# Low parts of weight chunks: an adding DMA in place of a subtraction, in one part of a dense fp32 kernel

## The chip, the cores and the metric

The kernel runs on one core of a Trainium2 chip. The metric is the device time of one execution in microseconds; lower is better. Three runs of the kernel before gave 2870.39 to 2872.4 us, median 2871.46 us.

## The reference

The reference sends 512 tokens of 1024 features through two blocks of two layers each, all in float32:

```
h = concat(meta, x)                            # 16 + 512 tokens
for l in (0, 1):                               # block 1
    z = rms_norm(h) @ w_in                     # projections
    ya = sliding-window attention with sinks (16 heads, window 128) * silu(gate)
    ym = mLSTM, 4 heads, normed, * sigmoid(o) * silu(gate)
    h = h + concat(ya, ym) @ w_out
x = h[16:]
for l in (0, 1):                               # block 2
    z = rms_norm(x) @ w_in_2
    a = differential attention, 8 heads; b = dilated attention, 3 groups of 4 heads
    c = attention over 256 memory tokens, 4 heads
    x = x + (gated sum of a, b, c through their own matrices) @ w_out_2
out = rms_norm(x) * g_final
```

Nearly all the arithmetic is in the products with the weights. They are needed to float32's precision.

## The kernel before

Features lie on the partitions and tokens along the free dimension. TensorE multiplies in float32r, a shorter form of float32, so each operand is taken as a sum of a high part (the value rounded to float32r) and a low part (what is left). A product is the sum of three: high times high, high times low, low times high.

A weight chunk is a tile of 128 partitions by 1024 words (512 KB), which serves 8 blocks of 128 by 128. There are 404 of them, and `weights()` prepares each one. SP loads the raw chunk (`wr`, two tiles in rotation), ACT casts it to the high part (`wh`, three tiles), and the low part (`wl`, three tiles) is raw minus high: on POOL for every third chunk (L184), on DVE for the others (L171, through `split`). `dense()` then runs, for a chunk, first the 16 steps that use `wh` and then the 8 that use `wl`; the steps have 512 columns in block 2 and two halves of 264 in block 1. `dense_tok()` does the same with the chunk as the moving operand.

A layer of block 1 has 50 chunks for its projections (`w1`) and 16 for its output (`wo1`). A layer of block 2 has 32 chunks up to the end of the differential heads, 40 for the dilated heads, and then 65 for the memory attention, the gates, the branch matrices and the output.

The attention's own pieces (scores, softmax, transposes, weighted values, evacuations) are generators that advance by a stage after every dense product. A scheduler in the framework then orders each engine's instructions by a timeline of its own; each engine runs its list in that order, and waits at an instruction whose inputs or whose buffer are not there yet. So an engine's list holds weight work and attention work mixed, and what stands behind a waiting instruction waits with it.

Names that come up: L458 and L957 score plus mask and its maximum (DVE), L470 and L986 the exponentials (ACT), L478, L989 and L990 the scaled weights (DVE), L486 and L943 their transposes (PE), L174 and L329 evacuations of PSUM (DVE), L1245/L1246 copies of key halves and L1007 squares (POOL).

Of the kernel before, what the change touches and what calls it, by code (L numbers as in the profile page):

```python
# [10 lines left out]
F32 = mybir.dt.float32  # L11
# [10 lines left out]
# attention of block 1: queries in blocks of 112, each sees 16 meta keys and a window of 240  # L22
# [4 lines left out]
# the order of the groups of four heads and of the mLSTM's heads  # L27
ORDER = [("a", 0), ("m", 0), ("a", 1), ("m", 1), ("a", 2), ("m", 2), ("a", 3), ("m", 3)]
# blocks of tokens of the mLSTM
# [4 lines left out]
# the evacuation of a product goes before this many instructions that were given earlier  # L34
AHEAD = 300
# rounds of the streams for each dense product: block 1's, its output projection's, block 2's (differential, other)
# [6 lines left out]
# the table of per-feature values and of rows that all partitions need  # L43
# [14 lines left out]
def turned(t):  # L58
    """the tokens of each tile in reverse order."""
    return tiles4(t)[:, :, ::-1]  # L60


class Kernel:
    def __init__(self, nc, tc, d, es):
# [12 lines left out]
        self.nw = 0  # chunks of weights so far  # L77

    # ------------------------------------------------------------ storage
# [4 lines left out]
    def slot(self, dt=F32, shape=None):  # L84
        """one of the slots of 528 words for each partition; release() names the last use."""
        i = self.idle.popleft()
        t = self.sp.tile(shape or [128, L1], dt, name=self.uid("s"), tag=f"s{i}")
        self.held[id(t)] = (i, t)
        return t
# [27 lines left out]
    # ------------------------------------------------------------ a software pipeline  # L117
    # What follows a dense product (posts) and the attention's pieces (units, in streams) are generators.
    # They advance by stages after every dense product, so that a stage's inputs are there when its turn comes.
    def post(self, gen):  # L120
        """starts now and goes on by a stage at every step."""
        self.posts.append(gen)
        self.advance(self.posts, [gen])
# [12 lines left out]
    def round(self, s):  # L136
        """the stream's active units go on by a stage, and the next one starts."""
# [14 lines left out]
    def drain(self, gens=None):  # L152
        """until these units have been through (None: all posts)."""
# [8 lines left out]
    # ------------------------------------------------------------ products  # L162
# [3 lines left out]
    def split(self, src, hi, lo, scale=None):  # L166
        """src * scale = hi + lo, both exact in float32r."""
# [8 lines left out]
    def weights(self, src):  # L176
        w = lambda tag, dt: self.wp.tile([128, 1024], dt, name=self.uid(tag), tag=tag, bufs=2 if tag == "wr" else 3)
        raw = w("wr", F32)
        self.nc.sync.dma_start(raw, src)
        hi, lo = w("wh", F32R), w("wl", F32R)  # L180
        self.nw += 1
        if self.nw % 3 == 1:
            self.nc.scalar.copy(hi, raw)  # L183
            self.nc.gpsimd.tensor_tensor(lo, raw, hi.bitcast(F32), ALU.subtract)  # L184
        else:
            self.split(raw, hi, lo)
        return hi, lo

    def dense(self, outs, chunks, xs, halves, ks=None):
        """outs[j] = sum over k of W_k^T x_k on the columns halves[j]: hi hi + hi lo + lo hi."""  # L190
# [8 lines left out]
    def dense_tok(self, chunks, xs, nt, vh, vl, rc):  # L199
        """256 columns of the product with tokens on partitions, scaled by rc, in two parts."""  # L200
# [13 lines left out]
    def rms_rows(self, r, acc, T, halves, n, exp=True):  # L214
        """r = 1/sqrt(acc summed over the partitions / n + eps), the same on all partitions; its log without exp."""
# [12 lines left out]
    def rsqrt(self, y, x, shape):  # L228
        """y = 1/sqrt(x) of small tiles: a guess from the exponent, then Newton's steps."""
# [10 lines left out]
    def columns(self, r, rc, n):  # L240
        """rc[t, i] = r[0, 128 i + t]; r is the same on all partitions."""
# [16 lines left out]
    def layer_input(self, st, m, x, T, g):  # L258
        """what the next layer needs of tile m of the residual: its parts times the gain, its squares."""
# [5 lines left out]
    def keep(self, name, m, x, T):  # L265
        """the residual waits in memory for the end of the layer."""
# [4 lines left out]
    def silu2(self, z, T):  # L271
        """z = 2 * silu(z)."""
# [6 lines left out]
    # ------------------------------------------------------------ constants  # L279
    def constants(self):  # L280
# [30 lines left out]
        # the mLSTM's first 16 tokens: the values' high | low | high parts at 0, 32, 64 with a column of ones  # L311
        # that the low parts lack, and the weights' high | high | low parts
# [9 lines left out]
    # ------------------------------------------------------------ block 1: attention  # L322
# [9 lines left out]
    def qk_parts(self, z, gcol):  # L332
        """the parts of z times the gain and those of its squares."""
# [8 lines left out]
    def rope(self, z, g, gcol):  # L342
        """z times the gain with the rotary embedding."""
# [11 lines left out]
    def a_keys(self, l, z, st):  # L355
        """each kv head's keys on both halves of the partitions, high parts and low parts."""
# [26 lines left out]
    def a_values(self, l, z, st):  # L383
        """values of each block's keys, tokens on partitions: [key, half, kv head, high 64 | low 64]."""
# [16 lines left out]
    def a_queries(self, l, z, sqs, qs):  # L401
        """two heads without their norm: each one's high parts and low parts side by side on the partitions."""
# [14 lines left out]
    def a_norms(self, sqs, rs):  # L417
        """rs[q, block, head] = the norm's factor and the attention's scale for four heads."""
# [16 lines left out]
        # 8 / sqrt(mean + eps) / 64  # L435
# [3 lines left out]
    def a_block(self, l, g, b, qs, rs, st, ya):  # L439
        """heads 4g .. 4g+3, a block of queries."""  # L440
# [65 lines left out]
    def a_gate(self, g, qs, ya, gates, st, ys):  # L506
        """after the five blocks of four heads: two gated tiles for ys."""
# [1046 lines left out]
```

## Time and profile before

| | |
|---|---|
| median of three runs | 2871.46 us |
| span of the profiled execution | 2868.8 us |
| PE busy | 2776.6 us (97%) |
| DVE busy | 1964.4 us (68%) |
| ACT busy | 1398.6 us (49%) |
| POOL busy | 728.2 us (25%) |
| DMA queue of SP | 248.82 MB, 26.3% of 16 engines |

The profiler gives the span from the first to the last instruction; no separate time of that execution is at hand. It lies 2.7 us below the median of the runs, so a difference of spans can be set on the median as it stands. PE's first matmul waits 9.7 us for the first inputs. The page's chain of work that ended last is 75% PE, 17% DVE and 4% ACT. DVE's load is uneven: about 90% in the first 400 us, about 35 to 45% in the output parts of block 2.

### The profile page before, as it was taken

The page shows a single profiled execution, that of the slowest core. Times are in us where ns is not written, and L with a number is a line of the kernel's source. Part 1 is how long each engine was busy: PE and PEld are TensorE (multiplying, and loading weights), DVE is VectorE, ACT ScalarE, POOL GpSimd, SP SyncE. Part 2 cuts the span into 40 slices and gives each one's busy share as a digit, 9 for nine tenths or more (in the row PEclk, how much of TensorE's full clock was granted, in tenths as well). Part 3 has the DMA queues.
Part 4 walks back from the last instruction along what each step waited for, and adds up shares of the span by engine and source line. Part 5 has one row for each costly group of instructions (what it writes and reads, how often), then busy time and mean ns, then how long its engine had stood idle before and what let it go on. Part 6 is the DMA issues. An engine that isn't in the chain of part 4 may idle for free.

```text
span 2868.8 us, 43625 instructions
## 1 busy us (share of the span) xinstructions
PE 2776.6 (97%) x16728; PEld 2446.4 (85%) x16728; DVE 1964.4 (68%) x4261; ACT 1398.6 (49%) x2649; POOL 728.2 (25%) x610
## 2 busy tenths in 40 slices
PE   7999999999999999999999999999998999999997
PEld 7999989999998878878898888888887888888886
DVE  6999886589889757778555772445777664674344
ACT  5555654556565445556443452234555543453223
POOL 5143322224323232221211211322221121211222
PEclk9999999999999999999999999999999999999998
DMA  3221213311111342222223312243221222322232
GB/s 133 67 67 60 67 54 106 116 67 67 61 66 67 113 133 87 80 72 86 89 68 100 122 67 96 99 137 109 80 79 65 87 88 77 110 91 79 96 125 74
DMA packets 96911, 251.60 MB, mean 88 GB/s; under 512 B 9374, under 2 KB 33638, under 8 KB 96574
## 3 DMA queue, kind: packets, MB, share of 16 engines
q1 hardware_dynamic: 96702, 248.82, 26.3%
q8 instruction: 131, 2.15, 0.3%
q14 instruction: 78, 0.64, 0.1%
HBM read 240.19 MB, written 8.60 MB: 87 GB/s over the span
## 4 chain that ended last, share of the span: by engine, by line
PE 75%; DVE 17%; ACT 4%; issue 2%; DMA 1%; SPq 0%; POOL 0%; DVEq 0%; ACTq 0%; POOLq 0%
PE z L164 54%; PE a L164 18%; DVE s L171 2%; DVE wl L171 2%; PE a L943 1%; PE a L486 1%; DVE s L413 1%; DVE s L458 1%; DVE s L329 1%; DVE s L174 1%; DVE s L478 1%; DVE s L276 1%; DVE s L957 1%; DVE s L990 1%; ACT s L470 1%
## 5 line engine op out<-in xcount | busy, mean ns | idle before, releaser
L164 PE MATMUL z<-s,wh 128*128 128x512 f32 (+2 forms) x6784 | 1268.7, 335 | 25.9 <-ACT s L173 9.7
L164 PEld LDWEIGHTS z<-s,wh 128*128 128x128 f32 x6784 | 1045.9, 190 | 159.9 <-ACT s L173 10.3
L164 PE MATMUL z<-s,wl 128*128 128x264 f32 (+2 forms) x3392 | 661.8, 333 | 0.0
L184 POOL TENSOR_TENSOR wl<-wr,wh 128x1024 fp32r<-128x1024 f32 x135 | 333.6, 2471 | 1246.9 <-PE z L164 623.7
L164 PEld LDWEIGHTS z<-s,wl 128*128 128x128 f32 x3392 | 526.5, 188 | 62.4
L170 ACT CAST wh<-wr 128x1024 fp32r<-128x1024 f32 x269 | 281.7, 1048 | 425.5 <-PE z L164 277.8
L164 PE MATMUL a<-s,s 128*128 128x512 f32 (+5 forms) x1900 | 426.6, 339 | 13.9 <-DVE t L458 8.0
L171 DVE TENSOR_TENSOR wl<-wr,wh 128x1024 fp32r<-128x1024 f32 x269 | 354.7, 1321 | 36.9 <-ACT wh L170 32.7
L164 PEld LDWEIGHTS a<-s,s 128*128 128x128 f32 (+1 forms) x1900 | 298.9, 188 | 50.8 <-DVE t L458 9.1
L1206 DVE TENSOR_TENSOR s<-z,s 128x512 f32<-128x512 f32 x128 | 88.0, 688 | 239.9 <-PE z L164 230.3
L183 ACT CAST wh<-wr 128x1024 fp32r<-128x1024 f32 x135 | 141.4, 1048 | 205.0 <-PE z L164 97.1
L171 DVE TENSOR_TENSOR s<-s,s 128x512 fp32r<-128x512 f32 (+6 forms) x272 | 211.7, 789 | 27.4 <-ACT s L170 24.4
L170 ACT CAST s<-s 128x512 fp32r<-128x512 f32 (+6 forms) x272 | 151.1, 567 | 140.3 <-DVE s L1208 26.5
L164 PE MATMUL z<-wh,s 128*128 128x256 f32 x1408 | 208.1, 286 | 5.4 <-DVE s L174 5.0
L164 PEld LDWEIGHTS z<-wh,s 128*128 128x128 f32 x1408 | 188.2, 192 | 14.5 <-DVE s L174 8.1
L171 DVE TENSOR_TENSOR s<-a,s 128x512 fp32r<-128x512 f32 (+3 forms) x266 | 149.8, 581 | 61.2 <-ACT s L170 60.2
L164 PE MATMUL a<-s,wh 128*128 128x512 f32 x768 | 188.2, 393 | 0.0
L170 ACT CAST s<-a 128x512 fp32r<-128x512 f32 (+3 forms) x266 | 127.2, 504 | 93.2 <-PE a L943 49.9
L164 PEld LDWEIGHTS a<-s,wh 128*128 128x128 f32 x768 | 144.0, 188 | 33.4
L957 DVE CUSTOM_DVE_ANT_0 s<-a,reg 128x512 f32<-128x512 f32 x160 | 107.4, 684 | 31.4 <-PE a L164 30.2
L986 ACT ACTIVATE s<-s,t 128x512 f32<-128x512 f32 x128 | 91.3, 715 | 56.7 <-DVE t L983 51.9
L164 PE MATMUL z<-wl,s 128*128 128x256 f32 x704 | 116.9, 284 | 0.0
(254 smaller groups left out, 3068.8 us busy)
## 6 DMA issues: line engine op xcount, KB each, us to landing
wr<-w SPq DMA_DIRECT2D x308, 512.0 KB, 3.5
wr<-wo SPq DMA_DIRECT2D x48, 512.0 KB, 3.4
wr<-wb SPq DMA_DIRECT2D x32, 512.0 KB, 3.5
reg<-tab SPq DMA_DIRECT2D x24, 448.0 KB, 3.5
s<-x SPq DMA_DIRECT2D x16, 264.0 KB, 4.1
r<-s SPq DMA_DIRECT2D x16, 256.0 KB, 2.0
wr<-wmk SPq DMA_DIRECT2D x8, 512.0 KB, 3.4
wr<-wmv SPq DMA_DIRECT2D x8, 512.0 KB, 3.9
```

What stands on the lines that cost most here:

```text
L164: self.nc.tensor.matmul(out, lhsT, rhs, start=start, stop=stop)
L170: nc.scalar.copy(hi, src)
L171: nc.vector.tensor_tensor(lo, src, hi.bitcast(F32), ALU.subtract)
L174: nc.vector.scalar_tensor_tensor(lo, src, scale, hi.bitcast(F32), ALU.mult, ALU.subtract)
L183: self.nc.scalar.copy(hi, raw)
L184: self.nc.gpsimd.tensor_tensor(lo, raw, hi.bitcast(F32), ALU.subtract)
L276: nc.vector.scalar_tensor_tensor(z[:, :T], th[:, :T], 1.0, z[:, :T], ALU.add, ALU.mult)
L329: self.nc.vector.tensor_tensor(two(z), ps[:, :, : u - t], two(r), ALU.mult)
L413: nc.vector.tensor_tensor(t[b], z[a], t[a].bitcast(F32), ALU.subtract)
L957: self.nc.vector.tensor_tensor_reduce(e, ps, bias[:, 3 - i : 7 - i].rearrange("p a b -> p (a b)"), 1.0, LOW, ALU.add, ALU.max, mx)
L986: nc.scalar.activation(es[m], es[m], AF.Exp, bias=mx[:, m : m + 1], accum_out=den[:, m : m + 1])
L1206: nc.vector.tensor_tensor(z[:, :512], ps, r[:, :512], ALU.mult)
```

## The change

`weights()` has two forms now, chosen by a flag `adding`. It is set after the first two chunks, cleared before the memory attention of each layer of block 2, and set again at the start of a block-2 layer. So 274 of the 404 chunks (130 of block 1, 72 of each layer of block 2) take the new form and 130 the old.

In the new form ACT writes minus the raw chunk, rounded to float32r, into the low part's tile; then a DMA issued from POOL reads the same chunk of weights from memory a second time and adds it into that tile, which leaves raw minus high; ACT's cast to the high part comes behind. The old form is as before (POOL for every third chunk, counted over these chunks alone).

The tiles in rotation become three raw (were two), three high, four low (were three). That takes 8 KB more of each partition; the space for descriptors of POOL's DMAs is set to 8192 bytes a partition. The rest of the diff removes comments and docstrings.

```
+        self.adding = False                       # __init__
     def weights(self, src):
-        w = lambda tag, dt: self.wp.tile([128, 1024], dt, name=self.uid(tag), tag=tag, bufs=2 if tag == "wr" else 3)
-        raw = w("wr", F32)
-        self.nc.sync.dma_start(raw, src)
-        hi, lo = w("wh", F32R), w("wl", F32R)
+        nc = self.nc
+        raw, hi, lo = (
+            self.wp.tile([128, 1024], dt, name=self.uid(t), tag=t, bufs=n) for t, dt, n in (("wr", F32, 3), ("wh", F32R, 3), ("wl", F32R, 4))
+        )
+        nc.sync.dma_start(raw, src)
+        if self.adding:
+            nc.scalar.mul(lo, raw, -1.0)
+            nc.gpsimd.dma_start(lo, src, accum_op=ALU.add)
+            nc.scalar.copy(hi, raw)
+            return hi, lo
+        nc.scalar.copy(hi, raw)
         self.nw += 1
-        if self.nw % 3 == 1:
-            self.nc.scalar.copy(hi, raw)
-            self.nc.gpsimd.tensor_tensor(lo, raw, hi.bitcast(F32), ALU.subtract)
-        else:
-            self.split(raw, hi, lo)
+        (nc.gpsimd if self.nw % 3 == 1 else nc.vector).tensor_tensor(lo, raw, hi.bitcast(F32), ALU.subtract)
         return hi, lo
...
     def layer2(self, l, st, nxt):
+        self.adding = True
...
+        self.adding = False
         mk, mv = self.mem_kv(l)
...
         w0 = self.weights(d["w1"][0, 0]), self.weights(d["w1"][0, 1])
+        self.adding = True
...
-    nc = bacc.Bacc("TRN2", target_bir_lowering=False, num_devices=1)
+    nc = bacc.Bacc("TRN2", target_bir_lowering=False, num_devices=1, dynamic_dma_scratch_size=8192)
```

Over the whole program PE and SP keep the same instructions. DVE loses 183 of its 269 subtractions `wl<-wr,wh`, POOL 91 of its 135; ACT gains 274 instructions `wl<-wr` (L186 in the changed file), POOL 274 DMAs `wl<-w` (L187). The scheduler orders every list anew. Lines of the changed file are 6 to 9 higher than those before.

DVE, first layer of block 2, where the fourth differential head's output ends and the next head's weights begin (`s_15366` and `s_15518` are the same tile of weights, before and after; `wl` is a weight chunk's low part). Before:

```order
L983 TENSOR_SCALAR t_15428<-t_15428 128x2
L988 TENSOR_TENSOR t_15365<-t_15365,t_13777 128x1
L1254 TENSOR_TENSOR s_15692<-s_15618,s_15692 64x512
L1015 SCALAR_TENSOR_TENSOR s_15318<-s_15318,s_15319 128x512
L983 TENSOR_SCALAR t_15488<-t_15488 128x2
L989 TENSOR_SCALAR s_15367<-s_15367,t_15365 128x512
L171 TENSOR_TENSOR wl_15927<-wr_15924,wh_15926 128x1024
L1016 TENSOR_TENSOR s_15318<-s_15318,s_14836 128x512
L987 RECIPROCAL t_15429<-t_15429 128x2
L990 SCALAR_TENSOR_TENSOR s_15366<-s_15366,t_15365,s_15367 128x512
```

And in the changed kernel, up to the same instruction (L996 now):

```order
L989 TENSOR_SCALAR t_15581<-t_15581 128x2
L994 TENSOR_TENSOR t_15517<-t_15517,t_13907 128x1
L963 ISA s_15645,t_15642<-a_15650,reg_13817 128x512
L963 ISA t_15642 128x1
L995 TENSOR_SCALAR s_15519<-s_15519,t_15517 128x512
L989 TENSOR_SCALAR t_15642<-t_15642 128x2
L996 SCALAR_TENSOR_TENSOR s_15518<-s_15518,t_15517,s_15519 128x512
```

The subtraction `wl` that stood three places ahead of the scaled weights is gone from the list; the score of a later tile (L963) stands there now.

ACT at the same place (L1014/L1020 and L986/L992 are the fourth head's norm and the next head's exponentials). Before:

```order
L223 ACTIVATE s_15319<-a_15348,eps 128x512
L173 ACTIVATE s_15695<-z_15699,t_13766 128x256
L1253 CAST s_15689<-s_15618 64x512
L1253 CAST s_15692<-s_15618 64x512
L1014 ACT_TABLE_LOAD
L1014 ACTIVATE s_15319<-s_15319 128x512
L170 CAST wh_15926<-wr_15924 128x1024
L986 ACTIVATE s_15430,t_15429<-s_15430,t_15428 128x512
L986 ACTIVATE s_15431,t_15429<-s_15431,t_15428 128x512
L986 ACTIVATE s_15490,t_15489<-s_15490,t_15488 128x512
```

In the changed kernel:

```order
L229 ACTIVATE s_15471<-a_15500,eps 128x512
L1020 ACT_TABLE_LOAD
L1020 ACTIVATE s_15471<-s_15471 128x512
L992 ACTIVATE s_15518,t_15517<-s_15518,t_15516 128x512
L992 ACTIVATE s_15519,t_15517<-s_15519,t_15516 128x512
L188 CAST wh_16084<-wr_16083 128x1024
L992 ACTIVATE s_15583,t_15582<-s_15583,t_15581 128x512
L992 ACTIVATE s_15584,t_15582<-s_15584,t_15581 128x512
L186 ACTIVATE wl_16193<-wr_16191 128x1024
L992 ACTIVATE s_15644,t_15643<-s_15644,t_15642 128x512
L992 ACTIVATE s_15645,t_15643<-s_15645,t_15642 128x512
```

Between the exponentials of one head there stood one weight instruction; now there are two, and one of them waits for a low tile that PE has let go.

POOL from the third to the fourth head's squares (L1007/L1013). Before:

```order
L1007 TENSOR_TENSOR s_15026<-s_15025 128x512
L184 TENSOR_TENSOR wl_15511<-wr_15508,wh_15510 128x1024
L1245 CAST s_15377<-s_15377 64x512
L1245 CAST s_15383<-s_15383 64x512
L1246 CAST s_15378<-s_15378 64x512
L1246 CAST s_15384<-s_15384 64x512
L184 TENSOR_TENSOR wl_15758<-wr_15755,wh_15757 128x1024
L1007 TENSOR_TENSOR s_15319<-s_15318 128x512
```

In the changed kernel:

```order
L1013 TENSOR_TENSOR s_15174<-s_15173 128x512
L187 DMA wl_15745<-w 128x1024
L1252 CAST s_15529<-s_15529 64x512
L1252 CAST s_15535<-s_15535 64x512
L1253 CAST s_15530<-s_15530 64x512
L187 DMA wl_15859<-w 128x1024
L1253 CAST s_15536<-s_15536 64x512
L187 DMA wl_15914<-w 128x1024
L1252 CAST s_15731<-s_15731 64x512
L1253 CAST s_15732<-s_15732 64x512
L1013 TENSOR_TENSOR s_15471<-s_15470 128x512
```

Two subtractions became three adding DMAs, and these stand between the copies of the keys; each waits for ACT's `wl<-wr`.

## Rows read from the trace of the kernel before

**Rows 1.** The page's first part: busy us, share of span, instructions by engine.
```profile
PE 2776.6 (97%) x16728; PEld 2446.4 (85%) x16728; DVE 1964.4 (68%) x4261; ACT 1398.6 (49%) x2649; POOL 728.2 (25%) x610
```
**Rows 2.** By stretch: length; busy PE, PEld, DVE, ACT, POOL; PEclk; DMA share; GB/s.
```profile
100.00:1055.00 955.00, 931.40 (x7017) 884.33 (x7016) 788.64 (x2089) 521.40 (x1140) 302.40 (x312) 0.99 0.24 78
1055.00:1565.00 510.00, 495.72 (x2710) 423.65 (x2709) 348.53 (x704) 265.16 (x476) 108.28 (x75) 0.99 0.26 84
...
1965.00:2455.00 490.00, 475.57 (x2610) 405.82 (x2610) 333.55 (x663) 249.81 (x447) 104.51 (x73) 0.99 0.25 82
```
**Rows 3.** PE's waits (total us, times, longest): first and last, 100:1055, 1055:1565, 1965:2455.
```profile
PE a L164 <- DVE t L458: 8.0, 10, 1.3
...
PE a L164 <- DVE s L719: 0.3, 1, 0.3
...
PE a L943 <- DVE s L990: 8.6, 4, 4.7
...
PE a L164 <- ACT s L170: 0.2, 1, 0.2
...
PE a L943 <- DVE s L990: 8.0, 5, 3.9
...
PE z L164 <- DVE s L1208: 0.5, 2, 0.3
```
**Rows 4.** DVE and PE around 1262 us, in time order: start, duration, engine, line, operation.
```profile
1261.39 1.22 DVE L171 TENSOR_TENSOR wl<-wr,wh 128x1024 fp32r<-128x1024 f32 x1
1263.20 0.73 DVE L990 SCALAR_TENSOR_TENSOR s<-s,t,s 128x512 f32<-128x512 f32 x1
1263.99 0.69 PE L943 MATMUL a<-ident,s 128*128 128x128 f32 x2 [4.68 <-DVE s L990]
```
**Rows 5.** Busy time in the 4.4 us before it, columns as in Rows 2.
```profile
1259.00:1263.40 4.40, 0.31 (x3) 0.10 (x1) 3.48 (x8) 4.39 (x10) 0.00 (x0) 1.00 0.23 66
```
**Rows 6.** Stretches at half clock: two of nine, and the nine's sum.
```profile
413.60:420.40 6.80, 5.56 (x23) 4.87 (x24) 6.57 (x26) 2.79 (x6) 0.00 (x0) 0.50 0.05 17
...
1263.50:1270.30 6.80, 5.04 (x21) 4.13 (x22) 5.01 (x12) 2.40 (x6) 0.00 (x0) 0.50 0.25 80
...
sum 40.80, PE 36.06 PEld 31.72 DVE 31.93 ACT 15.82 POOL 0.00; mean PE 4.01 PEld 3.52 DVE 3.55 ACT 1.76 POOL 0.00
```
**Rows 7.** Groups of the weight work and of dense steps: busy, mean ns | idle before.
```profile
L164 PE MATMUL z<-s,wh 128*128 128x512 f32 x2944 | 731.7, 396 | 6.6 <-DVE s L174 3.2 <-DVE s L1206 2.6 <-DVE s L1208 0.5
L171 DVE TENSOR_TENSOR wl<-wr,wh 128x1024 fp32r<-128x1024 f32 x269 | 354.7, 1321 | 36.9 <-ACT wh L170 32.7 <-PE z L164 3.6 <-ACT t L473 0.2
L184 POOL TENSOR_TENSOR wl<-wr,wh 128x1024 fp32r<-128x1024 f32 x135 | 333.6, 2471 | 1246.9 <-PE z L164 623.7 <-PE a L164 249.9 <-ACT wh L183 198.0
...
L183 ACT CAST wh<-wr 128x1024 fp32r<-128x1024 f32 x135 | 141.4, 1048 | 205.0 <-PE z L164 97.1 <-PE a L164 36.3 <-DMA wr<-w 36.0
```
**Rows 8.** DVE's subtractions, then ACT's casts, in the three stretches of adding chunks.
```profile
100.00:1055.00 955.00, 104.23 (x82) 0.99 0.24 78
1055.00:1565.00 510.00, 58.50 (x45) 0.99 0.26 84
...
1965.00:2455.00 490.00, 57.64 (x44) 0.99 0.25 82
...
100.00:1055.00 955.00, 127.81 (x122) 0.99 0.24 78
1055.00:1565.00 510.00, 72.22 (x69) 0.99 0.26 84
...
1965.00:2455.00 490.00, 69.74 (x67) 0.99 0.25 82
```
**Rows 9.** SP's issue of a chunk (ns), its landing (us), and the DMA queue.
```profile
L179 SPq DMA_DIRECT2D wr<-w x308: 327/328/425, 1.2 to 2776.6; - x154
...
wr<-w SPq DMA_DIRECT2D x308, 512.0 KB, 3.5
...
q1 hardware_dynamic: 96702, 248.82, 26.3%
```

## The prediction

> **What bounds the kernel now.** I read the page's busy shares first: PE is busy 97% of the span [rows 1], so at most the 92 us that PE idles and what slows it while it is busy can be won. Then the stretches in which chunks will take the new form: 100 to 1055 us (block 1), 1055 to 1565 and 1965 to 2455 us (differential and dilated heads of the two layers) [rows 2]. DVE's load is 788.6/955 = 0.83, 348.5/510 = 0.68 and 333.6/490 = 0.68 there, ACT's 0.55, 0.52 and 0.51. Then PE's waits in them [rows 3]: the ten rows of the first stretch add up to 21.7 us on DVE and 1.0 on ACT, the six of the second to 12.6 and 1.5, the seven of the third to 12.4 and 1.8; together 46.7 us on DVE and 4.3 on ACT. None is for a weight chunk: each is for a score, a scaled weight or an evacuation that stands late in DVE's list. The longest shows how [rows 4]: PE waits 4.68 us for the scaled weights of L990, and shortly before those DVE spends 1.22 us on a weight chunk's subtraction. But ACT too was busy for 4.39 of the last 4.40 us there [rows 5].
>
> Waits cost a second time. PE's clock is granted at half in nine stretches of these parts, 40.8 us in all, with PE busy for 36.1 us [rows 6]; one begins at 1263.5, in the wait just shown. [...]
>
> **DVE and POOL: what is removed.** DVE loses 183 subtractions of 1.321 us, 242 us; POOL loses 91 of 2.471, 225 us [rows 7]. Neither engine is the bound, so what counts is what stands in the way of PE's operands. I take the time that work spends behind other work on an engine as going with load/(1-load). That is a rule of thumb for a busy queue, not a row. With the subtractions out [rows 8], DVE's load becomes (788.6-104.2)/955 = 0.72, (348.5-58.5)/510 = 0.57 and (333.6-57.6)/490 = 0.56, and the factor falls from 4.74 to 2.53, from 2.16 to 1.32 and from 2.13 to 1.29. PE's waits on DVE then shrink to 0.53, 0.61 and 0.60 of what they were: 11.5 + 7.7 + 7.4 = 26.6 us, 20.1 less.
>
> **ACT: what is added.** 274 instructions `wl<-wr`, each as long as the cast beside it, 1.048 us [rows 7]: 287 us more. In the three stretches that doubles the casts' 127.8, 72.2 and 69.7 us [rows 8], and ACT's load becomes 0.68, 0.66 and 0.65. The same factor rises by some 1.8, so PE's waits on ACT go from 4.3 to 7.7 us, 3.4 more. What hides the 287 us is ACT's idle time, 434, 245 and 240 us in the three stretches before, of which 306, 173 and 171 are left. Behind a waiting `wl<-wr` stand the exponentials; it waits for the raw chunk and for a low tile that PE has let go. Its wait for PE should end earlier than that of the cast behind it: the tile of four chunks ago is let go at that chunk's end, the high tile of three chunks ago two thirds of a chunk later.
>
> **POOL and the DMA: what is added.** The trace shows no DMA issued from POOL and none that adds. The issue I bound from below by SP's 0.33 us [rows 9] and from above by the subtraction it replaces, 2.47 us [rows 7], and take 1 us, nearer the issue than the arithmetic. Over 274 chunks that is 90 to 677 us, 274 as taken, against the 225 that POOL gives back; POOL's 0.32, 0.21 and 0.21 of load [rows 2] bear either end. It stands in POOL's list among the copies of keys (L1245) and waits for ACT. POOL waited 623.7 us in all at its subtractions for PE [rows 7], and PE shows no wait for what stood behind them [rows 3].
>
> The transfer lands after 3.5 us when it only copies, and takes the 16 engines 0.263 x 2868.8 us / 248.82 MB x 0.524 MB = 1.6 us [rows 9]. Adding must read the tile as well as the source, so 1.6 to three times that, 4.8 us; I take 3.2. The landing I bound by 3.5 and, thrice, 10.5 us, and take 7. A chunk costs PE at least 24 x 731.7/2944 = 6.0 us [rows 7], on average 955/122 = 7.8 in block 1 and 7.3 in block 2 [rows 2, 8]. From the moment a low tile is let go to the first step that reads it again there are three chunks and two thirds, 22 us. ACT's 1.05, the issue and the landing need 9 us as taken, 14 with the upper ends. So I charge the new path nothing. What hides it is the extra low tile: with three tiles it would have 16 us. The engines' share grows from 26% by 274 x 3.2/2868.8 = 31 points.
>
> [...]
>
> **Third raw tile, descriptor space, subtracting chunks.** PE shows no wait on weights, so a deeper rotation has nothing to remove. The 130 chunks left keep their form. The bound is zero there, give or take the new order of the lists.
>
> **Sum.** 20.1 less on DVE, 3.4 more on ACT: 16.7 of 51.0 us, a third. A third of the 18 us at half clock, 5.9. Together 22.6: 2871.5 - 22.6 = 2849 us, a gain of 0.8%. Upper end of the gain: all 51 us of waits and the 18, 2802.
>
> **Rivals.** 1. *ACT takes DVE's place; slower.* The 4.39 of 4.40 us [rows 5] speak for it: the chain of scores, exponentials and scaled weights passes ACT, and what DVE delivers late may itself be late from ACT. If all of PE's 51 us of waits went with ACT's factor of 1.8, they would grow by 41 us and the half clock by 14; half of that gives 2871 + 27 = 2898, a quarter 2885. It decides once more than about 40% of the waits behind DVE's name are ACT's. Against it: ACT's load at 0.68 stays under DVE's at 0.83 of now, and only 4.3 of 51 us bear its name.
>
> 2. *The low parts come late; much slower.* If adding takes the DMA engines longer than the 7.3 us of a chunk less the 1.6 of its raw load, 5.7 us, PE is paced by them: at 7 us each, 274 x 1.3 = 356 us more, 3228; at 6 us, 82 us, 2953. Nothing in the trace excludes it, as no row adds; the room of 3.6 plain transfers speaks against it. [...]
>
> 3. *No change.* The lists are planned anew for a lighter DVE: L963 stands where the subtraction stood. If PE's waits are where the plan's times are off, not where DVE is loaded, new ones replace the old, and the time stays within 6 us of 2871.
>
> **How the numbers follow.** A measurement of this kernel can tell about 0.2%, 5.7 us, from no change. Forecast 0.64: its own range is 2825 to 2863, from two thirds of the 69 us gone, 46, to a ninth, 8. Rival 1 0.13, of which most lies under 2892. Rival 2 0.07. Rival 3 0.16. The range 2818 to 2890 leaves out rival 2, the worse part of rival 1 and a little at the fast end. Faster 0.64, same 0.16, slower 0.20.
>
> **What would show it.** DVE at 1964 - 242 = 1720 us busy or a little less, ACT at 1399 + 287 = 1686, POOL's 44 subtractions at 109 us; a new queue with 144 MB written. PE's waits on DVE in the stretches at 27 us, on ACT at 8; fewer than nine stretches at half clock. The step on ACT is wrong if PE waits for L992 or L476 (exponentials) or ACT's own list holds DVE up. The step on the DMA is wrong if PE waits for a `wl` or ACT waits long for one. The whole is wrong if DVE is lighter as said and PE's waits are not.

## The result and the profile after

The changed kernel takes 2823.59 us (median of four runs, 2822.53 to 2825.28) against 2871.93 us for the kernel before beside it: a ratio of 0.9835, 95% interval 0.9821 to 0.9849, 48 us less. The span of its profiled execution is 2820.8 us, also 48.0 less than before. The direction was as forecast; the gain is over twice the 22.6 us of the sum.

Page's first part and the three stretches of adding chunks, of the changed kernel (columns as in [rows 2]):

```profile
PE 2753.5 (98%) x16728; PEld 2435.9 (86%) x16728; DVE 1637.8 (58%) x4078; ACT 1653.4 (59%) x2923; POOL 697.6 (25%) x793
```
```profile
100.00:1040.00 940.00, 933.06 (x7126) 891.39 (x7124) 653.27 (x2012) 647.02 (x1269) 290.37 (x400) 1.00 0.66 151
1040.00:1540.00 500.00, 491.67 (x2695) 421.03 (x2694) 280.72 (x658) 320.64 (x540) 100.63 (x116) 0.99 0.67 156
1930.00:2410.00 480.00, 471.47 (x2600) 404.04 (x2599) 267.92 (x630) 310.07 (x519) 96.45 (x113) 1.00 0.68 155
```

DVE is 327 us lighter than in [rows 1], although the 183 subtractions taken from it were worth 242. ACT gained 255 us, and POOL is almost as busy as before. PE idles 67 us of the span where it idled 92. The longest of PE's waits in the first and second stretch (lines stand one to nine further down: L165 was L164, L996 was L990):

```profile
PE a L165 <- DVE s L509: 1.5, 2, 0.7
...
PE z L165 <- DVE s L175: 3.7, 5, 1.3
PE a L949 <- DVE s L996: 2.7, 3, 1.1
...
PE z L165 <- DVE s L1215: 0.6, 1, 0.6
```

The list of block 1 is headed by 1.5 us, where [rows 3] began with 8.0 for the scores. In all, PE's waits on DVE in the three stretches are 5.6, 7.0 and 7.2 us, 19.8 together, and on ACT 3.5; before they were 46.7 and 4.3. Half clock took 40.8 us in nine pieces of these stretches before [rows 6]; now it takes 10.2 us in two. The whole program has five such pieces after its start, two of them in the first 40 us. The two of the stretches, and the sum of the five:

```profile
1220.60:1227.40 6.80, 5.46 (x26) 5.36 (x26) 4.11 (x9) 2.49 (x7) 0.00 (x0) 0.50 0.60 152
...
2114.90:2118.30 3.40, 3.40 (x19) 3.40 (x18) 1.76 (x3) 2.06 (x4) 0.00 (x0) 0.50 0.34 67
sum 23.80, PE 19.24 PEld 18.27 DVE 15.20 ACT 13.44 POOL 6.51; mean PE 3.85 PEld 3.65 DVE 3.04 ACT 2.69 POOL 1.30
```

Where the time came from, by stage: from PE's first product to the first transposition to columns of block 2 (block 1) 1056.5 us before, 1020.9 after; then the layers of block 2, 900.1 to 894.0 and 889.7 to 884.4. Three quarters of the gain is in block 1. By kind, over the whole program: I set the time from each matmul's start to the next one's against the fast quarter of its shape before. Steps over 150 ns late at full clock sum to 87.0 us before and 59.5 after (-27.5). What is late at half clock, waits within it included, is 28.6 and 9.5 (-19.1). Small lateness is about 126 both times.

The weight work, and the DMA (queues, then landing; columns as in [rows 7] and [rows 9]):

```profile
L186 ACT ACTIVATE wl<-wr 128x1024 fp32r<-128x1024 f32 x274 | 288.6, 1057 | 92.4 <-PE z L165 88.9 <-PE a L165 3.0
L188 ACT CAST wh<-wr 128x1024 fp32r<-128x1024 f32 x274 | 286.9, 1047 | 313.4 <-PE z L165 308.4 <-PE a L165 4.5
L187 POOL DMA_DIRECT2D wl<-w x242 | 209.7, 867 | 1089.1 <-ACT wl L186 949.5 <-ACT s L1052 39.0 <-DVE s L1213 14.7
```
```profile
q0 software_dynamic: 39456, 143.67, 30.5%
q1 hardware_dynamic: 96702, 248.82, 26.2%
...
wl<-w POOLq DMA_DIRECT2D x242, 512.0 KB, 5.8
```

The issue of an adding DMA keeps POOL for 0.867 us, the transfer takes the engines 0.305 x 2820.8 / 274 = 3.1 us and lands after 5.8. No matmul waits for one.

### The profile page after: what moved, and what is told of

Its sections match the earlier page's. It is cut to its first block, busy times and chain, and to the rows that moved or that the text cites. A ratio compares the mean times of both kernels' runs of the same rounds, so it can differ in the third digit from the quotient of the medians.

```text
span 2820.8 us, 44127 instructions
## 1 busy us (share of the span) xinstructions
PE 2753.5 (98%) x16728; PEld 2435.9 (86%) x16728; DVE 1637.8 (58%) x4078; ACT 1653.4 (59%) x2923; POOL 697.6 (25%) x793
## 4 chain that ended last, share of the span: by engine, by line
PE 88%; ACT 6%; DVE 4%; issue 1%; DMA 1%; POOL 0%; DVEq 0%; ACTq 0%; SPq 0%
PE z L165 64%; PE a L165 20%; PE a L949 1%; PE a L492 1%; ACT s L992 1%; ACT wl L186 1%; ACT wh L188 1%; ACT L229 1%; DVE s L963 0%; ACT s L171 0%; ACT L1020 0%; DVE s L175 0%; DVE s L172 0%; ACT s L229 0%; ACT s L174 0%
## 5 line engine op out<-in xcount | busy, mean ns | idle before, releaser
L165 PE MATMUL z<-s,wh 128*128 128x512 f32 (+2 forms) x6784 | 1267.7, 334 | 27.1 <-ACT s L174 8.7
L165 PEld LDWEIGHTS z<-s,wh 128*128 128x128 f32 x6784 | 1045.1, 189 | 161.0 <-ACT s L174 8.9
L165 PE MATMUL z<-s,wl 128*128 128x264 f32 (+2 forms) x3392 | 657.8, 333 | 0.0
L165 PEld LDWEIGHTS z<-s,wl 128*128 128x128 f32 x3392 | 525.3, 188 | 62.7
L187 POOL DMA_DIRECT2D wl<-w x242 | 209.7, 867 | 1089.1 <-ACT wl L186 949.5
L165 PE MATMUL a<-s,s 128*128 128x512 f32 (+5 forms) x1900 | 420.3, 336 | 4.2 <-ACT s L171 1.7
L186 ACT ACTIVATE wl<-wr 128x1024 fp32r<-128x1024 f32 x274 | 288.6, 1057 | 92.4 <-PE z L165 88.9
L165 PEld LDWEIGHTS a<-s,s 128*128 128x128 f32 (+1 forms) x1900 | 295.4, 186 | 35.3 <-ACT s L171 5.1
L192 DVE TENSOR_TENSOR wl<-wr,wh 128x1024 fp32r<-128x1024 f32 x86 | 108.0, 1255 | 202.7 <-ACT wh L190 197.2
L172 DVE TENSOR_TENSOR s<-s,s 128x512 fp32r<-128x512 f32 (+6 forms) x272 | 189.1, 708 | 47.7 <-ACT s L171 40.4
L165 PE MATMUL z<-wh,s 128*128 128x256 f32 x1408 | 209.1, 286 | 7.8 <-DVE s L175 7.5
L192 POOL TENSOR_TENSOR wl<-wr,wh 128x1024 fp32r<-128x1024 f32 x44 | 106.0, 2410 | 438.4 <-ACT wh L190 336.1
L165 PEld LDWEIGHTS z<-wh,s 128*128 128x128 f32 x1408 | 188.0, 191 | 16.0 <-DVE s L175 11.1
L171 ACT CAST s<-s 128x512 fp32r<-128x512 f32 (+6 forms) x272 | 149.9, 565 | 79.2 <-PE a L165 15.5
L165 PE MATMUL a<-s,wh 128*128 128x512 f32 x768 | 188.8, 393 | 0.0
L165 PEld LDWEIGHTS a<-s,wh 128*128 128x128 f32 x768 | 144.0, 188 | 33.4
L171 ACT CAST s<-a 128x512 fp32r<-128x512 f32 (+3 forms) x266 | 126.1, 503 | 65.7 <-PE a L949 37.3
L963 DVE CUSTOM_DVE_ANT_0 s<-a,reg 128x512 f32<-128x512 f32 x160 | 108.0, 686 | 40.7 <-PE a L165 39.3
```

Of the source, the lines that this page charges most:

```text
L165: self.nc.tensor.matmul(out, lhsT, rhs, start=start, stop=stop)
L171: nc.scalar.copy(hi, src)
L172: nc.vector.tensor_tensor(lo, src, hi.bitcast(F32), ALU.subtract)
L186: nc.scalar.mul(lo, raw, -1.0)
L187: nc.gpsimd.dma_start(lo, src, accum_op=ALU.add)
L192: (nc.gpsimd if self.nw % 3 == 1 else nc.vector).tensor_tensor(lo, raw, hi.bitcast(F32), ALU.subtract)
```

## The experiments

Twelve kernels ran, each in five rounds against the kernel before on the same chip, in three sets; the kernel before had medians of 2869.3, 2869.8 and 2873.0 us in them, so medians of different sets compare to some 4 us. "The three parts" below are the additions in DVE's place, those in POOL's place, and the rotation (raw/high/low tiles: 2/3/3 before, 3/3/4 after).

### The rotation without the additions

```diff
-        if self.adding:
+        if False:
```

> All 404 chunks subtract as before; only the rotation is that of the change (three raw, four low tiles, 8192 bytes of descriptor space). Theory A (DVE's list gets shorter and PE's waits on DVE go): same as before, 2865 to 2876 us, PE's waits on DVE near 59 us. Theory B (POOL's subtractions stretch DVE's instructions while both run): the same. Theory C (the deeper rotation itself gives the gain): 2850 us or less.

Measured: 2888.5 us, ratio 1.0063 (1.0050 to 1.0075), 19 us slower than before. All three theories missed: the rotation by itself costs. (The descriptor space, 8192 bytes in all twelve kernels, is counted with it here; no run varies it.)

### Additions in POOL's place alone, and in DVE's place alone

Both with tiles 3/3/4, `self.nw += 1` moved ahead of the test, and the test changed:

```diff
+        if self.adding and self.nw % 3 == 1:   # first run: POOL's 91 chunks add
+        if self.adding and self.nw % 3 != 1:   # second run: DVE's 183 chunks add
```

> In the same part of the program only the 91 chunks whose low part POOL subtracted take the adding form; DVE keeps its 269 subtractions, ACT gains 91 instructions. Theory A: a small gain, 2858 to 2870 us, DVE busy near 1950. Theory B: half of the 48 us or more, 2848 us or less, and DVE busy about 80 to 110 us less than before without having lost an instruction.

> The other 183 chunks of that part take the adding form, POOL keeps all its 135 subtractions; DVE has the 86 subtractions that the changed kernel has. Theory A: most of the gain, 2824 to 2836 us, DVE busy near 1964 - 242 = 1722. Theory B: at most half of it, 2848 us or more, with DVE's other instructions as long as before.

Measured: 2859.5 us, ratio 0.9963 (0.9951 to 0.9976), and 2855.2 us, ratio 0.9946 (0.9933 to 0.9958). Against the same tiles without additions (2888.5) that is -29.0 for POOL's 91 chunks and -33.3 for DVE's 183. Their sum, -62.3, is close to the -64.9 of the changed kernel: the two parts add up, and a chunk of POOL's is worth nearly twice one of DVE's. By time the first run fell into its theory A and the second into its theory B, but both had reckoned from the kernel before and not from 2888.5. The first part of the page without additions, and with POOL's chunks adding, shows something I had no term for:

```profile
PE 2776.9 (96%) x16728; PEld 2446.8 (85%) x16728; DVE 1924.0 (67%) x4261; ACT 1399.6 (48%) x2649; POOL 715.4 (25%) x610
```
```profile
PE 2764.2 (97%) x16728; PEld 2441.3 (85%) x16728; DVE 1843.0 (65%) x4261; ACT 1486.7 (52%) x2740; POOL 564.1 (20%) x610
```

DVE has the same 4261 instructions and is 81 us less busy (121 less than before), with POOL's 91 subtractions gone; the run that puts them back, below, shows them as the cause.

### Which tile the additions need

The changed kernel with tiles 2/3/3, 3/3/3, 2/3/4 and 2/4/4, by this line alone:

```diff
-            ... for t, dt, n in (("wr", F32, 3), ("wh", F32R, 3), ("wl", F32R, 4))
+            ... for t, dt, n in (("wr", F32, 2), ("wh", F32R, 3), ("wl", F32R, 3))
```

> The changed kernel with the rotation of before: two raw, three high, three low tiles. If the path of a low part (ACT 1.06 us, issue 0.87, landing 5.8) fits into the 16 us that three tiles give, 2818 to 2832 us and no wait of PE for a low tile. If the rotation is what hides it: 2840 us or more, with ACT waiting longer at the low tile's buffer and POOL's copies late behind it.

> The changed kernel with three low tiles in place of four; three raw and three high tiles stay. It tells apart which extra tile carries the 19 us by which the adding kernel gets slower with two raw and three low tiles (2842.8 against 2823.6). Theory A (the fourth low tile: the adding way takes its low tile at the first cast and lets it go at the last product of the chunk, while the transfer that adds lands 6 to 8 us after its issue, so a low tile is held longer than the 16 us that I had worked out): 2836 to 2843, and matmuls wait on the adding transfer (a row PE z <- DMA wl of over 8 us). Theory B (the third raw tile: the load, 3.9 us, then two casts by ACT behind its other work; with two raw tiles the next load starts late): 2822 to 2828. Theory C (the extra tiles act through the order of the lists alone): somewhere in 2822 to 2845 with no row of waits on the adding transfer.

> The changed kernel with two raw tiles in place of three; three high and four low tiles stay. The counterpart of the run with three low tiles. Theory A (the fourth low tile carries the 19 us): 2822 to 2828. Theory B (the third raw tile carries them): 2836 to 2843, with matmuls waiting on the transfers of the chunks. Theory C (both are needed, either one is short without the other): both runs at 2832 to 2840.

> The changed kernel with two raw, four high and four low tiles, as much memory as three, three and five would not need: one raw tile turned into a high tile. Theory A (the low tile is the late one and the high parts are in time with three): 2815 to 2823, as with two raw, three high and four low. Theory B (ACT's casts to the high tile wait for the last product of the chunk three back, and stand ahead of exponentials in ACT's list): 2805 to 2815. Theory C (a deeper rotation of any tile costs in the lists, as the third raw tile does): 2823 to 2835.

Measured, with the low tiles from three to four down the table:

| raw/high/low | us | ratio to before |
|---|---|---|
| 2/3/3 | 2842.75 | 0.9907 (0.9892 to 0.9923) |
| 3/3/3 | 2836.5 | 0.9880 (0.9866 to 0.9893) |
| 3/3/4 (the change) | 2823.59 | 0.9835 (0.9821 to 0.9849) |
| 2/3/4 | 2818.69 | 0.9820 (0.9806 to 0.9833) |
| 2/4/4 | 2821.1 | 0.9822 (0.9809 to 0.9836) |

The fourth low tile carries it: 24 us with two raw tiles, 13 with three. The third raw tile and a fourth high tile give nothing that these intervals can tell. With three low tiles, and either number of raw ones, matmuls wait for the adding transfer and it lands later (2/3/3, then 3/3/3; two views each):

```profile
PE z L165 <- DMA wl<-w: 12.5, 14, 2.4
...
wl<-w POOLq DMA_DIRECT2D x242, 512.0 KB, 7.9
```
```profile
PE z L165 <- DMA wl<-w: 8.1, 8, 2.3
...
wl<-w POOLq DMA_DIRECT2D x242, 512.0 KB, 7.9
```

With 2/4/4 it also lands after 7.9 us and no matmul waits, so the landing alone isn't it: with a fourth low tile there is time for it. The 2.3 to 2.4 us of the longest wait is how much the path was short.

### The fourth low tile without the additions

Tiles 2/3/4 and all chunks subtracting:

> All chunks subtract, with two raw, three high and four low tiles: the kernel before with a fourth low tile and no third raw tile. The third raw tile with a fourth low one made the subtracting kernel 19 us slower (2888.5). Theory A (the third raw tile does that: the next load and cast run further ahead, DVE's and POOL's lists hold a subtraction earlier and what is urgent stands behind it): 2864 to 2874 here, no change from before. Theory B (the fourth low tile does it, since a free low tile lets the subtractions be planned earlier): 2882 to 2892. Theory C (any change of the lists moves the time by some 15 us in either direction, with no rule): outside both.

Measured: 2885.4 us, ratio 1.0048 (1.0034 to 1.0061), 12 us slower than before. So the third raw tile is not needed to slow the subtracting kernel; what is left is the fourth low one (or the descriptor space, which no run separates from it). The changed kernel's tiles and the best ones, with no chunk adding, are thus 19 and 12 us worse than before, and with 274 adding 48 and 51 better. The loss lies in block 2 alone: block 1 is 3 us faster than before in both, the two layers of block 2 are 9 and 13 us slower with 3/3/4 and 15 and 4 with 2/3/4. Why, is open. In [rows 7] DVE idles 36.9 us in front of its subtractions; here it idles nearly ten times as long:

```profile
L192 DVE TENSOR_TENSOR wl<-wr,wh 128x1024 fp32r<-128x1024 f32 x269 | 336.3, 1250 | 338.7 <-ACT wh L190 314.2 <-issue 20.9 <-POOL s L1253 2.3
```

With a low tile free early, the scheduler puts the subtraction right behind the cast, and DVE's list stands there until ACT delivers. That reads like the cause, but it isn't borne out: of the 80.5 us in PE's gaps over 300 ns only some 8 lie within 3 us of such a halt, though such times cover a third of the span.

### POOL's subtractions put back beside the additions

```diff
             nc.scalar.copy(hi, raw)
+            self.nw += 1
+            if self.nw % 3 == 1:
+                nc.gpsimd.tensor_tensor(raw, raw, hi.bitcast(F32), ALU.subtract)
             return hi, lo
```

> The changed kernel with POOL's subtractions put back beside the additions: at every third adding chunk POOL subtracts the finished high part from the raw tile in place (91 instructions of 128x1024, result unused, nothing added to DVE or ACT). Theory A (POOL's two-input work stretches DVE's two-input instructions, which is why DVE's busy time fell 327 us where the 183 subtractions taken away are 242): DVE's busy time rises by 80 to 120 us with the same instructions, and the time by 8 to 25 us. Theory B (DVE's instructions got shorter for another reason, such as the lists that were planned again or fewer waits inside them): DVE's busy time within 25 us of 1638, time 2822 to 2832 (the raw tile is held a little longer).

Measured: 2868.05 us, ratio 0.9991 (0.9982 to 0.9999). Ninety-one instructions on an engine that is busy a quarter of the time, whose result nobody uses, cost 44 us, nearly the whole gain and far more than the 8 to 25 expected. DVE, with the same 4078 instructions, is 117 us busier:

```profile
PE 2769.7 (97%) x16728; PEld 2442.9 (85%) x16728; DVE 1754.8 (61%) x4078; ACT 1653.0 (58%) x2923; POOL 919.2 (32%) x884
```

How, can be seen at one of the 91, in order of time (start, duration, engine, line):

```profile
348.17 2.40 POOL L191 TENSOR_TENSOR wr<-wr,wh 128x1024 f32<-128x1024 f32 x1 [1.66 <-ACT wh L188]
348.42 0.56 DVE L700 SCALAR_TENSOR_TENSOR s<-a,s 128x384 f32<-128x384 f32 x1 [0.27 <-PE a L165]
348.91 0.77 DVE L359 TENSOR_TENSOR s<-a,reg 128x264 f32<-128x264 f32 x2
...
349.60 1.54 DVE L172 TENSOR_TENSOR s<-s,s 128x528 fp32r<-128x528 f32 x1
```

POOL works from 348.17 to 350.57. The DVE instructions that take one operand from PSUM (`a`) run beside it in 0.56 us and 0.77 us for two, close to the means of their shapes in the change, 0.54 and 0.42 each. The one with both operands in SBUF takes 1.54 us, where its shape's mean in the change is 0.73, and ends at 351.14, 0.57 us behind POOL's end. The trace of before, where POOL subtracts 135 times, shows the same whenever DVE begins; here two of DVE's own subtractions, one begun 0.20 us ahead of the end of POOL's, one 0.41 us behind its start:

```profile
1503.24 2.42 POOL L184 TENSOR_TENSOR wl<-wr,wh 128x1024 fp32r<-128x1024 f32 x1 [21.82 <-ACT wh L183]
...
1505.46 1.28 DVE L171 TENSOR_TENSOR wl<-wr,wh 128x1024 fp32r<-128x1024 f32 x1
...
1794.06 2.41 POOL L184 TENSOR_TENSOR wl<-wr,wh 128x1024 fp32r<-128x1024 f32 x1 [6.17 <-PE a L164]
...
1794.47 3.08 DVE L171 TENSOR_TENSOR wl<-wr,wh 128x1024 fp32r<-128x1024 f32 x1
```

Both end 1.08 us behind POOL, as do all 18 that begin under a subtraction of POOL (1.08 to 1.09). The 10 of `s<-s,s` with 512 columns that do so (L171) end 0.55 us behind it, the 5 TENSOR_SCALAR `t<-t` of two columns 0.02; 7 RECIPROCAL of the same shape end ahead of it. The 105 with a PSUM operand that begin under one are at most 16 ns longer than the fast fifth of their line and shape. So when these SBUF forms end goes by POOL's end and not by their own start.

### The control: POOL as busy, but only writing

```diff
+                for n in (1024, 1024, 512):
+                    nc.gpsimd.memset(raw[:, :n], 0.0)
```

in place of the subtraction of the last run.

> The control to the run with POOL's subtractions put back (2868.1, DVE 1754.8 us busy): at the same 91 chunks POOL works as long on the same raw tile after the same cast, but only writes (three memsets of 1024, 1024 and 512 columns, by the trace's 539 ns for 528 columns some 2.5 us a chunk), result unused. Theory A (a POOL instruction that reads SBUF and a DVE instruction with two inputs in SBUF exclude each other for their whole length, and that is what cost the 44 us): DVE's busy time within 40 us of 1638, as nothing reads, and the time 2822 to 2836. Theory B (the cost was POOL's time in front of its adding DMAs, or the raw tile held longer): DMAs as late as with the subtractions, 2850 to 2870. Theory C (any work of POOL in SBUF shuts DVE out, written or read): DVE at 1720 or more, 2850 to 2870.

Measured: 2837.7 us, ratio 0.9880 (0.9867 to 0.9894), DVE busy 1672.7 us, POOL 917.7 (the subtraction run: 919.2). With POOL as busy, 30 of the 44 us are gone once it no longer reads. Shapes of DVE in the changed kernel, with POOL's subtractions back, and with memsets:

```profile
L172 DVE TENSOR_TENSOR s<-a,s 128x512 fp32r<-128x512 f32 x112 | 74.4, 687 | 46.0 <-ACT s L171 45.6
L172 DVE TENSOR_TENSOR s<-s,s 128x512 fp32r<-128x512 f32 x99 | 73.2, 743 | 24.8 <-ACT s L171 21.8 <-PE a L165 3.0
L484 DVE TENSOR_SCALAR s<-s,t 128x256 f32<-128x256 f32 x160 | 48.7, 364 | 0.8
```
```profile
L172 DVE TENSOR_TENSOR s<-s,s 128x512 fp32r<-128x512 f32 x99 | 88.4, 896 | 26.6 <-ACT s L171 26.6
L172 DVE TENSOR_TENSOR s<-a,s 128x512 fp32r<-128x512 f32 x112 | 74.4, 686 | 53.5 <-ACT s L171 52.9
L487 DVE TENSOR_SCALAR s<-s,t 128x256 f32<-128x256 f32 x160 | 69.7, 495 | 0.7
```
```profile
L172 DVE TENSOR_TENSOR s<-s,s 128x512 fp32r<-128x512 f32 x99 | 74.9, 761 | 24.0 <-ACT s L171 23.9
L172 DVE TENSOR_TENSOR s<-a,s 128x512 fp32r<-128x512 f32 x112 | 74.3, 686 | 54.8 <-ACT s L171 54.2
L488 DVE TENSOR_SCALAR s<-s,t 128x256 f32<-128x256 f32 x160 | 64.4, 462 | 0.7
```

With a PSUM operand: 687, 686, 686 ns. With two SBUF operands: 743, then 896, then 761. The scaling with one SBUF operand is held up by both: 364, 495, 462. The memset time lies just over the upper end given by theory A, for a reason that the stages show: in block 1 the subtractions cost 17.0 us and the memsets nothing (-0.6), in the first layer of block 2 13.2 and 1.9, in the last one 12.2 and 12.1. Those 12 us of the last layer come whether the added work reads or not. Some 5 of them come at one place, in the memory attention, where no chunk adds and no memset runs:

```profile
2542.19 1.08 PE L953 MATMUL a<-ident,s 128*128 128x128 f32 x4 [3.61 <-DVE s L1136]
```

L1136 stands behind a subtraction and other work in DVE's list there, all at their usual lengths, with POOL idle, and 6.8 us at half clock begin in the wait. The run with the subtractions has the same wait of 3.6 us (L1135), the change has none. So a few microseconds of both runs come with the order of the lists and not with what POOL did at the time; the rest is open.

### Two versions that might be faster still

Additions for all chunks but the first two (the line that clears the flag taken out), and tiles 2/3/4 with all subtractions left on DVE:

```diff
-        self.adding = False
         mk, mv = self.mem_kv(l)
```
```diff
-        (nc.gpsimd if self.nw % 3 == 1 else nc.vector).tensor_tensor(lo, raw, ...)
+        nc.vector.tensor_tensor(lo, raw, ...)
```

> The changed kernel with the additions kept on to the end of both block-2 layers (memory attention, the last output projections and the chunks of the layer after it): all chunks but the first two add, none of DVE's and POOL's 129 subtractions stay. Theory A (the gain goes with the load of DVE and POOL taken away; 274 chunks gave 48 us, and a chunk of the subtracting part is worth as much): 2805 to 2818. Theory B (the rest has no need: in that part DVE and POOL are not what ends the waits, and ACT, which gets 128 more casts, is nearer to its limit): 2822 to 2835. Rival 1 of the prediction (ACT becomes the late one) would show here first: ACT's waits at PE over 30 us, time over 2835.

> A version that may beat both: tiles as in the run with two raw tiles (2818.7) and all subtractions that are left on DVE, none on POOL. DVE gets 44 more of 1.25 us, 55 us; POOL loses 106. Theory A (POOL's subtractions cost more by the DVE instructions that they shut out than they save): 2808 to 2818, DVE busy 1650 to 1685. Theory B (in this part the engines have room, nothing changes): 2816 to 2822. Theory C (DVE's load is what counts, as I had reckoned it in the prediction): 2822 to 2832.

Measured: 2835.06 us (0.9878, 0.9862 to 0.9893) and 2821.91 us (0.9828, 0.9815 to 0.9841). Adding everywhere loses 11 us against the change, all in block 2, though DVE falls to 1529 us. The values of the memory come by adding transfers that land after 10.1 us, and matmuls wait for them; PE's waits for ACT's L174 are 5.8 us longer than in the change (8.7):

```profile
PE z L165 <- ACT s L174: 14.5, 3, 9.2
PE z L165 <- DVE s L175: 12.5, 16, 1.4
PE z L165 <- DMA wl<-wmv: 7.0, 6, 2.2
```

Taking the last 44 subtractions off POOL is no gain over 2818.69 us. The best median of the study is the change with two raw tiles, 2818.69 us; its lead of 5 us over the change is within what the two intervals leave open.

## Why the prediction was right in direction and half the size

**The step that failed is the first: taking POOL's 91 subtractions away was put at nothing for PE.** The term took DVE's load as lighter by its own subtractions only, and POOL's were costed by what POOL gave back ("Neither engine is the bound, so what counts is what stands in the way of PE's operands"). But POOL's subtractions did stand in the way, through DVE: taking them out was worth 29.0 us beside the 33.3 of DVE's, and putting them back cost 44, of which 30 go with their reading.

In the sum, "PE's waits on DVE then shrink to 0.53, 0.61 and 0.60 of what they were: 11.5 + 7.7 + 7.4" was mis-sized in block 1, where 5.6 us are left, a quarter of the 21.7 before. The right load would not have saved it: DVE's load there is 0.69 (forecast 0.72), and with it load/(1-load), the author's estimate and shown by no trace, gives 10.4. In block 2 the totals came out, 7.0 and 7.2 us, but partly by luck: the waits for L990 fell to a third (8.6 and 8.0 to 2.7 each), and those for L174, L175 now, grew (3.4 and 2.2 to 3.7 and 3.8). Of the 25.7 us by which the measured gain exceeds the sum, DVE's waits make 6.8 (26.9 less, forecast 20.1), ACT's 4.2 (0.8 less, forecast 3.4 more), and the half clock 7.7 to 13.2, by the count below.

The trace of before shows how POOL stands in the way, here in block 2: while POOL subtracts, from 1191.16 to 1193.71, PE waits for L990, two instructions of some 0.75 us that take 3.50 together (the first alone 2.84).

```profile
1191.16 2.55 POOL L184 TENSOR_TENSOR wl<-wr,wh 128x1024 fp32r<-128x1024 f32 x1 [5.74 <-ACT wh L183]
...
1191.42 3.50 DVE L990 SCALAR_TENSOR_TENSOR s<-s,t,s 128x512 f32<-128x512 f32 x2
...
1194.32 0.44 PE L943 MATMUL a<-ident,s 128*128 128x128 f32 x2 [2.40 <-DVE s L990]
```

Counting DVE instructions that overlap a POOL subtraction and are over 100 ns longer than the fast fifth of their line and shape, before has 106 of them, 154 us in excess, the change 13 with 15. I had taken no relief from POOL; this one is large enough for DVE's fall by 327 and not 242. Of the 66.1 us in PE's gaps over 300 ns before, 23.5 lay within 3 us of a DVE instruction so held for over 300 ns; after, 3.9 of 42.9. So some 20 of the 23 us that these gaps lost were beside one. The run with the subtractions back, and its control, show it as a cause: in block 1 17 us, half of the 35.6 gained there, come back with the subtractions and none with the memsets.

Which of DVE's instructions it touches, the three shapes show: PSUM operand 687 ns in the change and 686 in both runs, two SBUF operands 743, then 896 under subtractions and 761 under memsets, one SBUF operand 364, 495 and 462. Why the form with one SBUF operand is longer even beside memsets, no run shows. The forecast did not look at the subtractions for this.

**The half clock: "A third of the 18 us at half clock, 5.9".** Counted as the forecast did, by half of PE's busy time at half clock in the stretches, 18.0 us became 4.4 (half of 5.46 + 3.40): 13.6 less. By the late steps of the whole program it is 19.1 less. Either way it fell more than the waits in proportion, which came down to less than half. The late steps at full clock (27.5 less) and the half clock (19.1) make 46.6 of the 48.0. The waits listed in the stretches fell by 27.7, forecast 16.7. The 18 us takes PE's work at half clock as doubled in length, which no run shows: in the trace of before eight matmuls of 256 columns take 2.08 us in a stretch at half clock and 1.11 us 5 us earlier, 1.87 times as long, by which the 36.1 us of [rows 6] hold 16.8 us of loss:

```profile
1190.33 1.11 PE L164 MATMUL z<-wh,s 128*128 128x256 f32 x8
...
1195.37 2.08 PE L164 MATMUL z<-wh,s 128*128 128x256 f32 x8
```

Of the nine stretches of before eight begin in a gap of PE of over 0.3 us or at most 1.3 us behind one; the one at 1055.3 does not.

**ACT: "3.4 more".** The work came as reckoned, 288.6 us for 274, and ACT's loads are 0.69, 0.64 and 0.65 (forecast 0.68, 0.66, 0.65). But waits on ACT went down, 4.3 to 3.5. So the rival in which ACT takes DVE's place is out for the whole. ACT's busy 4.39 of 4.40 us [rows 5] did hold DVE up there, but once and for less than a microsecond of the 4.68 that PE waited:

```profile
1260.32 0.69 DVE L1015 SCALAR_TENSOR_TENSOR s<-s,s 128x512 f32<-128x512 f32 x1 [0.92 <-ACT s L1014]
```

**The adding DMA: "I charge the new path nothing".** Right for the change: issue 0.87 us (taken 1), engines 3.1 us (taken 3.2), landing 5.8 us (taken 7), and no wait. The rival of late low parts shows up only with three tiles: by "with three tiles it would have 16 us", against a path of 9, the room should have been enough, and going without the fourth costs 13 to 24 us. In block 1 the room was there: with 3/3/3 the median from the last use of a low tile to its next is 21 us, and the low part lands 10.7 us ahead (chunks matched by their order). The waits lie in block 2, all 8 with 3/3/3 and 13 of 14 with 2/3/3. At the longest ones, at 1932 us of both traces, ACT waits for PE to let go of the tile, and PE wants it again 6.9 us later, not 16; the path takes 9.2 and 9.3. So the room was mis-sized at single places, which a time per chunk does not show.

**"So a deeper rotation has nothing to remove. … The bound is zero there".** It failed in both directions: without additions the rotation costs 12 to 19 us, with them the fourth low tile brings 13 to 24. The parts taken apart: additions with the old tiles -27 us against the kernel before beside them (2842.75, close to the forecast of 2849, but for reasons that I had not named), the rotation another 19 to 21.

**No change because the lists are planned anew.** Out for the whole. But what the runs leave open, the subtracting kernels with more tiles and the last layer under memsets, has a size of 6 to 20 us; that the new order of the lists makes it is likely, and shown only for the wait at L1136.

## What to carry to other kernels

Before moving work to an engine that is idle, look at what it holds up while it runs: compare the means of one shape with operands in SBUF and in PSUM (with POOL's subtractions back 896 ns against 743, and 686 against 687), and look for instructions of DVE that end just behind one of POOL. Removing 225 us of POOL's two-operand work was worth nearly as much here as 242 us of DVE's (29.0 against 33.3 us). And change the number of tiles together with the path that uses them: a fourth low tile was a loss for one path (12 us) and up to half of the gain for the other (24 us).

## What the runs showed of the hardware that I had not expected

Where POOL subtracted one SBUF tile from another, DVE's instructions with two SBUF operands that began meanwhile ended a fixed time behind it (1.08 us for 1024 columns, 0.55 for 512, in before), and those with a PSUM operand took at most 16 ns longer. With 91 such subtractions of 2.48 us put back DVE was busy 117 us longer, 1.3 us for each; with memsets in their place 35 us longer. Of these 35 us 23.6 are in the scalings with one SBUF operand (L484, L995, L1063 and L1064 of the change), 5.0 in L989 (`t<-t`, two columns) and 12.4 in L175 (`s<-s,s`, 16 instructions of 685 ns in the change, 1460 with memsets); the others together are 6 us shorter. L175 has 1470 ns in before too, where its seven long ones, some 2.47 us each, all begin under a subtraction of POOL between 2697 and 2798 us; for the memset run no row shows what lengthened it. An adding DMA of 512 KB cost 3.1 us of the 16 engines, twice a plain load's 1.6 [rows 9], and 0.87 us of POOL. Its landing was 5.8 us with tiles 3/3/4 and 2/3/4 and 7.9 with 2/3/3, 3/3/3 and 2/4/4, with the same bytes. The traces show what goes with it: an adding DMA in whose flight SP's queue takes less than 1 us of each engine lands after some 5.5 us in every kernel of the table, one with over 1.5 us after 7.0 to 8.6 (medians). In the change 98 of 274 are of the first kind, with three low tiles 6 (3/3/3) and 9 (2/3/3). A longer flight also meets more of SP's packets, so this is a link and not yet a cause.
